# The causal mask added by GpSimd and the gate as the bias of four exponentials, in the recurrence of a two-layer block

## The chip, the cores and the metric

One core of a Trainium2 chip runs the whole program. The metric is device time in microseconds (us) of one launch, over several runs. The engines have the names of the profile: PE is TensorE (matmuls), PEld its weight loads, DVE is VectorE, ACT is ScalarE, POOL is GpSimd, SP the queue that issues nearly all DMAs.

## The reference, cut to what matters

Layer 0 is attention over 256 context tokens and 1024 latents, layer 1 an mLSTM in both directions of time. The change is in layer 1's recurrence, which goes over chunks of 128 tokens:

```python
def step(carry, xs):
    C, n, m = carry
    qq, kk, vv, ig, fg = xs
    b = jnp.cumsum(fg, axis=-1)
    ...
    logD = jnp.where(tril, b[..., :, None] - b[..., None, :] + ig[..., None, :], -jnp.inf)
    m_t = jnp.maximum(b + m[..., None], jnp.max(logD, axis=-1))
    Dm = jnp.exp(logD - m_t[..., None])
    inter = jnp.exp(b + m[..., None] - m_t)
    sqk = jnp.einsum('bhtd,bhsd->bhts', qq, kk) * Dm
    num = jnp.einsum('bhts,bhsd->bhtd', sqk, vv) + inter[..., None] * jnp.einsum('bhde,bhte->bhtd', C, qq)
    den = jnp.sum(sqk, axis=-1) + inter * jnp.einsum('bhd,bhtd->bht', n, qq)
```

The weight `Dm` of key s for query t is exp(g_s - M_t) where s may be seen from t and 0 elsewhere, with g = ig - b and M the running maximum. `qq`, `kk` and `vv` are split into a high and a low part for the products that need precision.

## The kernel before

The recurrence (`phase_b`) works on 32 units: 8 heads times 4 pairs of chunks of the latents, and in a unit on 4 tiles of 128 keys by 128 queries (2 directions d, 2 chunks a). Per unit and in this order the program is written as

- `mid`: the weights times the values (`po<-vh,Eh`, `po<-vl,Eh`, `po<-vh,El`, in `mm3`, L77 to L79) and the state's share (`po<-C,q`, L1262), collected in `num` by ACT (L1258) and DVE (L1263);
- `states`: the chunks' keys and values into the states of the next head: transposes of `x` (`S<-idn,x`, L1205), `ah` high on ACT (L1168) and low on DVE (L1169), products `pc`, the states' update on DVE (L1186);
- a quarter of the next head's output gate (`wh`, `wl` split on POOL, `po<-wh,hT11h` on PE);
- `front` of the unit that follows: q times x (`S<-q,x`, L1229), the load of the negated maxima -M (`nM<-negM_d`, L1234, two DMAs that copy one row to all partitions), the weights E, and their split into Eh and El on POOL (L62, L66);
- `combine` (L1275 to L1289: `e` and `num` on POOL, `r` and `num` on DVE, `num` on ACT, `ms` on POOL) and, a unit later, `back` (transposes of `num`, L1301; `x` on ACT L1304, on DVE L1305, on POOL L1306, then the store `u_d<-x` on SP).

In `front`, before the change, DVE makes `E = min(nM + g, mask)` in four instructions (L1239), with the mask 0 or -1e30, and ACT one exponential over all four tiles (L1242); then DVE multiplies by the scores in PSUM (L1244: mul). `nM` and `E` are tiles with one buffer each: the next unit's `nM` can be loaded only when the last reader of the present one is done, and the next unit's `E` written only when POOL has read the present one for El.

No order is written by hand here. The program is given in the order above, and a scheduler puts each engine's instructions in a fixed order ahead of the run; on the chip each engine, and SP's queue of DMAs, then works strictly through its own list, and a waiting instruction holds all that stand behind it.

Of the kernel before, what the change touches and what calls it, by code (L numbers as in the profile page):

```python
# [19 lines left out]
P = 128  # L20
# [23 lines left out]
# the chunks in the order of each direction: the context first  # L44
# [5 lines left out]
class Ops:  # L50
    """The engines' short forms that the phases share."""
# [20 lines left out]
    def mm3(self, out, lhs, rhs, start, stop):  # L72
        """One step of an accumulated product of two split operands."""
        lh, ll = lhs
        rh, rl = rhs
        mm = self.nc.tensor.matmul
        mm(out, lh, rh, start=start, stop=False)  # L77
        mm(out, lh, rl, start=False, stop=False)  # L78
        mm(out, ll, rh, start=False, stop=stop)  # L79

    def rsqrt(self, out, ms):
        """out = (ms + EPS) ** -0.5"""
        self.nc.gpsimd.tensor_scalar(out, ms, 1.0, EPS, ALU.mult, ALU.add)
        self.nc.gpsimd.tensor_tensor(out, out, self.nhalf[: out.shape[0], : out.shape[1]], ALU.pow)


class Tokens:
    """Features by tokens, as hi and lo, in two tiles of tokens."""
# [12 lines left out]
class Stream:  # L101
    """Tiles of [P, D] in rotation, for the weights and the like of several phases: raw, and split as (hi, lo)."""
# [9 lines left out]
    def pair(self, hold=False):  # L112
        """hold: not to be handed out again before release()."""
# [12 lines left out]
class Modulation0:  # L126
    """Layer 0's cols [P, 2, KT, 2]: A and shift with features on partitions, for (latents, context).

    Parts j of 512 columns, of the shift (0, 1) and of the scale (2, 3)."""
# [16 lines left out]
    def sums(self, j):  # L146
        """The part's sums per partition, on the vector engine; finish() adds them up."""
# [9 lines left out]
    def product(self, j):  # L157
        """The part on the tensor engine."""
# [25 lines left out]
def modulation_rest(nc, ops, A, consts, dst, sp, raw, pair, psum, which):  # L184
    """dst[i]: rows [3, 2, D] in DRAM of layer i: A = norm_pre * (1 + scale), shift, gate * norm_post, for (latents, context).

    Per (i, j) in which two steps for columns j * 512 of shift | scale | gate: the sums on the vector engine, and the rest."""
# [38 lines left out]
def load_row(nc, pool, dst, which, s, name):  # L226
    """A row of the modulation (s: 0 latents, 1 context) on all partitions."""
# [5 lines left out]
def norm_rate(nc, ops, wp, y2, xt):  # L233
    """rsqrt of the rows' mean squares; y2 is written over."""
# [14 lines left out]
def norm(nc, ops, wp, xt):  # L249
    """The rows' rmsnorm."""  # L250
# [12 lines left out]
def shifted(nc, ops, y, shift, hT, f=slice(0, KT)):  # L263
    """hT (hi, lo) = y + shift, of the features' tiles f."""
# [5 lines left out]
def prenorm(nc, ops, wp, xt, row_a, row_s, eng):  # L270
    """rmsnorm(xt) * A + shift"""
# [7 lines left out]
def turn_T(nc, ops, pp, y2, hT, consts):  # L279
    """hT (hi, lo) = transpose of y2."""  # L280
# [3 lines left out]
def layer0(nc, tc, ops, A, consts, mod, dp, ahead, dbg):  # L284
    with ExitStack() as es:
# [10 lines left out]
        with ExitStack() as e1:  # L296
# [4 lines left out]
            with ExitStack() as e2:  # L301
# [18 lines left out]
                def at(t0, n):  # L320
                    """Tokens t0 to t0 + n of the normed input, hi and lo; the first latents lie apart from the others."""
# [101 lines left out]
            def gate(f, wg, wp):  # L423
                """Features f of the gate, on partitions."""
# [11 lines left out]
            with ExitStack() as e2:  # L436
# [11 lines left out]
                def rotary_key():  # L448
                    """The shared rotary key; [hi | lo] of its weights side by side."""
# [67 lines left out]
def queries(nc, ops, A, cT, q_d, g, wp, qp, psum, tab, qf_bufs):  # L517
    """Steps of the queries of heads 4 g to 4 g + 3, into q_d: features of a head lie in steps of four there."""
# [35 lines left out]
def attention(nc, tc, ops, A, consts, cT, kr_d, gate_d, oT_d, last, projected, q_d):  # L554
    """last: what is left to do before it, beside the first head's projections; projected: to be done after the last's."""
    with ExitStack() as es:
# [24 lines left out]
        def proj_v(h):  # L581
            """Values of heads h to h + 3: per head [hi | lo]."""
# [19 lines left out]
        def proj_k(h):  # L602
            """Keys of heads h and h + 1 without the rotary part, which stays in place."""
# [25 lines left out]
        def scores(h, b):  # L629
            """Pieces of a block of 256 queries: scores, and exponentials over their sums, context keys first."""  # L630
# [7 lines left out]
            def part(a, S, j, n):  # L638
                """Exponentials of a part of the keys against its own maximum, and their sum."""
# [22 lines left out]
            def weights(a):  # L662
                """The parts over the sum of all, brought to the largest of their maxima."""
# [20 lines left out]
        def values(h, b, st):  # L684
            """Pairs of steps per two tiles of keys: the transposed weights, and their product with the values."""
# [39 lines left out]
        def projections(h):  # L725
            """Steps beside the head before h."""
# [59 lines left out]
class Out0:  # L786
    """Layer 0's output projection, its norm and residual, and layer 1's normed input, transposed."""
# [13 lines left out]
    def load_o(self, tok, ks):  # L801
        """k-tiles of the first tiles of tokens, or of one."""
# [10 lines left out]
    def ahead(self, W, oT_d):  # L813
        """The first operands."""
# [4 lines left out]
    def run(self, hT, late, following):  # L819
        """late: pools for the last tiles' transposes, which are returned to be done later; following: the next loads."""  # L820
# [3 lines left out]
        with ExitStack() as es:  # L824
# [20 lines left out]
            # while the matrix arrives, three tiles side by side  # L845
# [36 lines left out]
def post(nc, ops, sp, ps, gn, xt, bufs=2, eng="pool"):  # L882
    """xt += rmsnorm(ps) * gn"""
# [9 lines left out]
def feature_weights(nc, ops, W, src):  # L893
    """One tile of features' weights, split."""
# [7 lines left out]
def phase_a(nc, tc, ops, A, consts, mod, hT, S, W, graw, wx0, late):  # L902
    """Layer 1's features: conv branch, its query form, values, and the gates' rows.

    wx0: the first weights; late: the step that completes the last tiles of hT."""
    with ExitStack() as es:
# [26 lines left out]
        for f in range(NF):  # L933
# [5 lines left out]
            # xm, features on partitions  # L939
# [40 lines left out]
            # gates  # L980
# [10 lines left out]
            # values, tokens on partitions  # L991
# [8 lines left out]
            # query form: q against raw conv features as keys  # L1000
# [7 lines left out]
            # the branch gate, for the latents alone  # L1008
# [9 lines left out]
def output_gate(nc, ops, A, S, hT, pools, g, tiles):  # L1018
    """Layer 1's output gate, before its function: steps of a head's weights, and of tiles of latents."""
# [21 lines left out]
def phase_z(nc, tc, ops, A, hT, S, W, tiles):  # L1041
    """Layer 1's output gate, for the latents' first tiles."""
# [583 lines left out]
```

## Time and profile before

| | |
|---|---|
| three runs, us | 2352.1, 2354.07, 2359.23 (median 2354.07) |
| profiled execution: span from first to last instruction | 2352.7 us; its time around the span isn't given |
| instructions | 38304 |
| busy over the span | PE 95%, PEld 83%, DVE 69%, ACT 52%, POOL 47% |
| the recurrence with units of all kinds | about 1687 to 2165 us |
| granted TensorE clock, mean | 0.987 of full speed |

A page of the profile gives busy time and the costliest groups of instructions; the views behind it give, for a stretch, the busy time of each engine, the instructions in order of time, and which engine or DMA ended each wait. "L1239" is line 1239 of the kernel before. Shares over the whole span are means over stages with different limits: in the recurrence alone DVE, not only PE, is busy nearly all the time.

### The profile page before, as it was taken

What the parts mean: (1) busy time and instruction counts of PE and PEld (TensorE: products, weight loads), DVE (VectorE), ACT (ScalarE), POOL (GpSimd) and SP (SyncE); (2) the same over time, 40 slices, a digit from 0 to 9 for tenths busy, and PEclk for the clock granted to TensorE, in tenths of its full rate; (3) what the DMA queues carried; (4) which work ended last, traced back from release to release, by engine and by line L of the source; (5) the groups of instructions that cost most, each with busy time, mean ns of one, the idle gap of its engine ahead of it and who ended that gap; (6) DMA issues with size and microseconds to landing.
All of it is one profiled execution on the core that took longest, in us unless ns stands there. A gap on an engine that the chain in (4) does not pass through costs nothing. (4 is left out here: it accounts for less than half of the span.)

```text
span 2352.7 us, 38304 instructions
## 1 busy us (share of the span) xinstructions
PE 2237.1 (95%) x13462; PEld 1952.1 (83%) x13462; DVE 1620.2 (69%) x3106; ACT 1212.1 (52%) x2935; POOL 1101.9 (47%) x1444
## 2 busy tenths in 40 slices
PE   8998999999999999999999999997999999997998
PEld 4877788998998998887878888887988888896787
DVE  5588499898898997467643444436298999997321
ACT  3512488888788886333222222233366677675111
POOL 3323356656656665562221111145546666656321
PEclk9999999999999999999999999999999999999999
DMA  7066422222311212543443333333634555545531
GB/s 260 28 210 219 142 79 78 71 59 67 88 45 58 82 54 89 178 157 124 137 144 117 126 115 109 111 132 103 208 106 152 161 163 173 169 124 177 171 125 54
DMA packets 189464, 292.26 MB, mean 124 GB/s; under 512 B 14108, under 2 KB 134812, under 8 KB 188888
## 3 DMA queue, kind: packets, MB, share of 16 engines
q1 hardware_dynamic: 188744, 287.97, 38.7%
q8 instruction: 107, 1.75, 0.3%
q0 software_dynamic: 528, 1.84, 0.2%
q14 instruction: 85, 0.70, 0.1%
HBM read 199.13 MB, written 90.62 MB: 123 GB/s over the span
## 5 line engine op out<-in xcount | busy, mean ns | idle before, releaser
L677 POOL TENSOR_SCALAR P<-P,sc,rs 128x512 f32<-128x512 f32 (+1 forms) x384 | 271.0, 720 | 160.4 <-DVE rs L675 109.1
L643 ACT ACTIVATE P<-S,nm 128x512 f32<-128x512 f32 (+1 forms) x416 | 254.2, 613 | 55.4 <-DVE nm L642 45.2
L642 DVE TENSOR_REDUCE nm<-S 128x1 f32<-128x512 f32 (+1 forms) x416 | 236.7, 578 | 19.8 <-PE S L79 18.8
L66 DVE TENSOR_TENSOR PTl<-tps,PTh 128x512 fp32r<-128x512 f32 x336 | 227.9, 680 | 10.5 <-ACT PTh L58 8.4
L58 ACT CAST PTh<-tps 128x512 fp32r<-128x512 f32 x336 | 197.0, 587 | 27.1 <-PE tps L694 24.3
L694 PE MATMUL tps<-idn,P 128*128 128x128 f32 x1344 | 202.0, 273 | 1.0 <-DVE PTl L66 0.7
L62 POOL TENSOR_SCALAR wh<-raw 128x512 fp32r<-128x512 f32 (+1 forms) x96 | 85.9, 907 | 242.0 <-PE xps L78 165.0
L66 DVE TENSOR_TENSOR wl<-raw,wh 128x1024 fp32r<-128x1024 f32 (+2 forms) x51 | 77.4, 1526 | 148.4 <-POOL wh L62 136.4
L694 PEld LDWEIGHTS tps<-idn,P 128*128 128x128 f32 x1344 | 156.5, 141 | 7.2 <-issue 1.0
L705 PEld LDWEIGHTS po<-PTh,V 128*128 128x128 f32 x672 | 119.3, 190 | 31.1 <-ACT o L714 11.4
L705 PE MATMUL po<-PTl,V 128*128 128x256 f32 x672 | 136.4, 284 | 7.5 <-DVE PTl L66 6.5
L1262 PE MATMUL po<-C,q 128*128 128x258 f32 x512 | 136.2, 388 | 6.1 <-ACT num L1258 6.1
L705 PE MATMUL po<-PTh,V 128*128 128x256 f32 x672 | 139.1, 288 | 2.7 <-ACT o L714 2.4
L77 PE MATMUL xps<-hT10h,wh 128*128 128x512 f32 (+1 forms) x384 | 139.4, 363 | 0.0
L78 PE MATMUL xps<-hT10l,wh 128*128 128x512 f32 (+1 forms) x384 | 137.4, 358 | 0.0
L79 PE MATMUL xps<-hT10h,wl 128*128 128x512 f32 (+1 forms) x384 | 137.3, 358 | 0.0
L974 DVE SCALAR_TENSOR_TENSOR xc<-xp,cw,xc 128x1282 f32<-128x1282 f32 x64 | 105.9, 1655 | 12.7 <-ACT xc L972 11.2
L705 PEld LDWEIGHTS po<-PTl,V 128*128 128x128 f32 x672 | 104.8, 189 | 9.0 <-DVE PTl L66 7.8
L1262 PEld LDWEIGHTS po<-C,q 128*128 128x128 f32 x512 | 89.9, 194 | 15.1 <-ACT num L1258 6.9
L1186 DVE SCALAR_TENSOR_TENSOR C<-C,decay,pc 128x258 f32<-128x258 f32 x224 | 100.1, 472 | 2.3 <-PE pc L79 2.0
L77 PE MATMUL xps<-hT11h,wh 128*128 128x512 f32 x256 | 99.9, 391 | 1.1 <-ACT hT11h L58 1.1
L79 PE MATMUL xps<-hT11h,wl 128*128 128x512 f32 x256 | 100.2, 391 | 0.0
(658 smaller groups left out, 7306.6 us busy)
## 6 DMA issues: line engine op xcount, KB each, us to landing
raw<-in_w_og SPq DMA_DIRECT2D x32, 512.0 KB, 4.2
qT<-q_d SPq DMA_DIRECT2D x16, 960.0 KB, 6.6
adaw<-in_ada_w SPq DMA_DIRECT2D x48, 256.0 KB, 3.3
q_d<-qs SPq DMA_DIRECT2D x24, 512.0 KB
xt<-in_xcat SPq DMA_DIRECT2D x20, 512.0 KB, 3.6
v_d<-vt SPq DMA_DIRECT2D x16, 640.0 KB
v<-v_d SPq DMA_DIRECT2D x40, 256.0 KB, 3.6
x<-xcT_d SPq DMA_DIRECT2D x40, 256.0 KB, 3.7
```

Source lines behind the costliest of these rows:

```text
L58: self.nc.scalar.copy(out, x)
L66: e.tensor_tensor(out, x, hi.bitcast(F32), ALU.subtract)
L77: mm(out, lh, rh, start=start, stop=False)
L78: mm(out, lh, rl, start=False, stop=False)
L79: mm(out, ll, rh, start=False, stop=stop)
L642: nc.vector.tensor_reduce(nm, S, axis=AX.X, op=ALU.max, negate=True)
L643: nc.scalar.activation(p, S, AF.Exp, bias=nm, accum_out=sm)
L677: nc.gpsimd.tensor_scalar(pt[j], pt[j], sc[:, j : j + 1], r[:, 3:], ALU.mult, ALU.mult)
L694: nc.tensor.transpose(pt[:, kk * 256 + a * P : kk * 256 + (a + 1) * P], src, consts["idn"])
L705: nc.tensor.matmul(po, Vs[h][:, k].rearrange("p a d -> p (a d)"), PT[i][:, kk * 256 : kk * 256 + 256], start=k == 0 and i == 0, stop=k == ...
L974: nc.vector.scalar_tensor_tensor(xc, xp[:, j : j + CONV_W], cw[:, f, j : j + 1], xc, ALU.mult, ALU.add)
L1262: nc.tensor.matmul(pi[:, :VW], qa, C[:, k], start=k == 0, stop=k == 1)
```

## The change

DVE's four instructions are gone. POOL adds the mask to -M, in place and for all four tiles at once (the mask is read twice by a broadcast), and ACT makes four exponentials of one tile each, with the column of g as the bias. The values are the same: a masked place has exp(-1e30) = 0. The rest of the diff only takes comments and docstrings away.

```diff
             nM = lp.tile([P, 2, U], F32, name="nM", bufs=1)
             for d in range(2):
                 nc.sync.dma_start(nM[:, d], S["negM"][d, h : h + 1, c * U : (c + 1) * U].partition_broadcast(P))
+
+            nv = nM.rearrange("p d (a s) -> p d a s", a=2)
+            nc.gpsimd.tensor_tensor(nv, nv, mask.unsqueeze(2).to_broadcast([P, 2, 2, P]), ALU.add)
             E = lp.tile([P, 2, 2, P], F32, name="E", bufs=1)
             for d in range(2):
                 for a in range(2):
                     gcol = cols[d][:, 2 * c + a, 3, h : h + 1]
-                    nc.vector.scalar_tensor_tensor(
-                        E[:, d, a], nM[:, d, a * P : (a + 1) * P], gcol, mask[:, d], ALU.add, ALU.min
-                    )
-            nc.scalar.activation(E, E, AF.Exp)
+                    nc.scalar.activation(E[:, d, a], nv[:, d, a], AF.Exp, bias=gcol)
             wide = ps[:, :, :P].unsqueeze(1).to_broadcast([P, 2, 2, P])
             nc.vector.tensor_tensor(E, wide, E, ALU.mult)
```

In the lists below a number behind a tile's name tells one tile of that name from another.

POOL's list between El of a head's last unit (El_21418) and the split of the next head's first (Eh_21604). Before:

```order
L66 TENSOR_TENSOR El_21418<-E_21410,Eh_21417 128x512
L66 TENSOR_TENSOR vl_21404<-v_20196,vh_21403 128x516
L1306 TENSOR_TENSOR x_20422<-x_20422,sz_21443 128x512
L1200 MEMSET v_21912 128x2
L1201 MEMSET v_21912 128x2
L1275 COPY e_21827<-gcol0_17373 128x2
L1275 COPY e_21827<-gcol1_17374 128x2
L1284 TENSOR_TENSOR num_21243<-num_21243,og_21421 128x256 x2
L62 TENSOR_SCALAR Eh_21604<-E_21597 128x512
L66 TENSOR_TENSOR El_21605<-E_21597,Eh_21604 128x512
```

And now:

```order
L66 TENSOR_TENSOR El_21418<-E_21411,Eh_21417 128x512
L1306 TENSOR_TENSOR x_20422<-x_20422,sz_21443 128x512
L66 TENSOR_TENSOR vl_21404<-v_20196,vh_21403 128x516
L1237 TENSOR_TENSOR nM_21809<-nM_21809,mask_18583 128x512
L1275 COPY e_21827<-gcol0_17373 128x2
L1275 COPY e_21827<-gcol1_17374 128x2
L1200 MEMSET v_21912 128x2
L1201 MEMSET v_21912 128x2
L1284 TENSOR_TENSOR num_21243<-num_21243,og_21421 128x256 x2
L83 TENSOR_SCALAR ms_21423<-ms_21423 128x2
L84 TENSOR_TENSOR ms_21423<-ms_21423,nhalf_67 128x2
L62 TENSOR_SCALAR Eh_21604<-E_21598 128x512
```

The add that is put in belongs to the unit after the one whose Eh follows (nM_21809 is for a later E than E_21598), it stands three rows behind El, and `ms` has moved ahead of Eh.

The same list behind El of a head's first unit (El_20747), where a quarter of the output gate's weights (`wh2`, `wl2`) is split. Before:

```order
L66 TENSOR_TENSOR El_20747<-E_20739,Eh_20746 128x512
L83 TENSOR_SCALAR ms_20565<-ms_20565 128x2
L84 TENSOR_TENSOR ms_20565<-ms_20565,nhalf_67 128x2
L66 TENSOR_TENSOR vl_20733<-v_20181,vh_20732 128x516
L1200 MEMSET v_21282 128x2
L1201 MEMSET v_21282 128x2
L62 TENSOR_SCALAR wh2_20794<-raw_20793 128x512 x2
L1306 TENSOR_TENSOR x_19579<-x_19579,sz_20772 128x512
L66 TENSOR_TENSOR wl2_20795<-raw_20793,wh2_20794 128x512 x2
L1275 COPY e_21212<-gcol0_17373 128x2
L1275 COPY e_21212<-gcol1_17374 128x2
L1284 TENSOR_TENSOR num_20598<-num_20598,og_20750 128x256
```

And now:

```order
L66 TENSOR_TENSOR El_20747<-E_20740,Eh_20746 128x512
L1306 TENSOR_TENSOR x_19579<-x_19579,sz_20772 128x512
L66 TENSOR_TENSOR vl_20733<-v_20181,vh_20732 128x516
L1237 TENSOR_TENSOR nM_21194<-nM_21194,mask_18583 128x512
L62 TENSOR_SCALAR wh2_20794<-raw_20793 128x512 x2
L1200 MEMSET v_21282 128x2
L1201 MEMSET v_21282 128x2
L1275 COPY e_21212<-gcol0_17373 128x2
L1275 COPY e_21212<-gcol1_17374 128x2
L66 TENSOR_TENSOR wl2_20795<-raw_20793,wh2_20794 128x512 x2
L1284 TENSOR_TENSOR num_20598<-num_20598,og_20750 128x256 x2
```

Again the add stands behind `x` and `vl`, with the gate weights' splits and `num` behind it.

DVE's list around `x_20179<-S_21232` (L1305), whose end frees a PSUM buffer, in a head's last unit. Before:

```order
L1283 SCALAR_TENSOR_TENSOR num_21000<-num_21000,r_21211 128x256
L1169 SCALAR_TENSOR_TENSOR ahl_21143<-v_21039,gcol1_17374,ahh_21142 128x258
L1239 SCALAR_TENSOR_TENSOR E_21410<-nM_21407,gcol0_17373,mask_18583 128x128 x2
L1239 SCALAR_TENSOR_TENSOR E_21410<-nM_21407,gcol1_17374,mask_18583 128x128 x2
L1305 SCALAR_TENSOR_TENSOR x_20179<-S_21232,hns_18585,x_20179 128x256 x2
```

And now:

```order
L1186 SCALAR_TENSOR_TENSOR C9_21094<-C1_20911,decay_17375,pc_21087 128x258
L1283 SCALAR_TENSOR_TENSOR num_21000<-num_21000,r_21211 128x256 x2
L1169 SCALAR_TENSOR_TENSOR ahl_21128<-v_21054,gcol0_17373,ahh_21127 128x258
L1305 SCALAR_TENSOR_TENSOR x_20179<-S_21232,hns_18585,x_20179 128x256 x2
L1186 SCALAR_TENSOR_TENSOR C6_21109<-C13_21079,decay_17375,pc_21102 128x258
```

The four L1239 that stood ahead of L1305 are gone, and one L1169 and one L1186 have moved behind it.

## Rows read from the trace of the kernel before

**Rows 1.** Stretches: length; busy us of PE, PEld, DVE, ACT, POOL; clock; DMA share:

```profile
1687.00:2165.00 478.00, 437.19 (x3025) 402.74 (x3025) 434.69 (x929) 323.01 (x807) 299.92 (x435) 0.98 0.52 158
1750.00:2100.00 350.00, 328.78 (x2340) 306.70 (x2339) 327.62 (x711) 246.97 (x630) 229.74 (x344) 0.99 0.53 161
1903.25:1923.48 20.23, 19.32 (x143) 17.82 (x141) 17.18 (x39) 12.86 (x31) 14.43 (x25) 1.00 0.53 187
1923.48:1934.57 11.09, 8.52 (x63) 7.98 (x62) 10.99 (x25) 8.66 (x24) 6.04 (x10) 1.00 0.42 108
1934.57:1945.10 10.53, 10.53 (x79) 10.05 (x79) 10.33 (x25) 6.14 (x17) 6.46 (x10) 1.00 0.47 141
1945.10:1960.88 15.78, 15.20 (x108) 14.11 (x107) 15.35 (x33) 12.49 (x31) 11.69 (x18) 1.00 0.67 195
```

**Rows 2.** What PE waited for, 1750 to 2100 us (total, times, longest):

```profile
PE S L1205 <- issue: 10.8, 5, 2.6
PE po L77 <- DVE num L1263: 4.0, 7, 0.6
PE pc L79 <- DVE thl L66: 2.9, 5, 0.6
```

**Rows 3.** Groups of DVE, 1687 to 2165 us: busy us, mean ns | idle before:

```profile
L1169 DVE SCALAR_TENSOR_TENSOR ahl<-v,gcol,ahh 128x258 fp32r<-128x258 f32 x141 | 88.1, 627 | 7.9 <-PE S L1205 4.5 <-ACT ahh L1168 3.1
L1239 DVE SCALAR_TENSOR_TENSOR E<-nM,gcol,mask 128x128 f32<-128x128 f32 x127 | 60.4, 530 | 1.3 <-DMA nM<-negM_d 1.0 <-POOL El L66 0.4
```

**Rows 4.** Line 1239 alone: duration ns min/median/max:

```profile
L1239 DVE SCALAR_TENSOR_TENSOR E<-nM,gcol,mask x128: 334/340/4407, 1686.4 to 2144.0; 128x128 f32<-128x128 f32 x128
```

**Rows 5.** In order of time, DVE and PE, 1924 to 1927 us (start, us):

```profile
1924.56 1.51 DVE L1239 SCALAR_TENSOR_TENSOR E<-nM,gcol,mask 128x128 f32<-128x128 f32 x4
1925.99 0.86 DVE L1305 SCALAR_TENSOR_TENSOR x<-S,hns,x 128x256 f32<-128x256 f32 x2
...
1926.96 0.41 PE L1205 MATMUL S<-idn,x 128*128 128x128 f32 x2 [2.57 <-issue]
```

**Rows 6.** In order of time, POOL and DVE, near 1902 us:

```profile
1901.97 1.27 POOL L66 TENSOR_TENSOR El<-E,Eh 128x512 fp32r<-128x512 f32 x1
...
1902.40 1.13 DVE L1169 SCALAR_TENSOR_TENSOR ahl<-v,gcol,ahh 128x258 fp32r<-128x258 f32 x1 [0.20 <-ACT ahh L1168]
```

**Rows 7.** Groups of ACT, whole span: busy us, mean ns:

```profile
L643 ACT ACTIVATE P<-S,nm 128x512 f32<-128x512 f32 x256 | 178.4, 697 | 39.4 <-DVE nm L642 37.4 <-DVE rs L675 0.4
L643 ACT ACTIVATE P<-S,nm 128x256 f32<-128x256 f32 x160 | 76.2, 478 | 16.0 <-DVE nm L642 7.7 <-PE tps L694 5.8 <-DVE rs L673 0.8
L1242 ACT ACTIVATE E<-E 128x512 f32<-128x512 f32 x32 | 20.2, 631 | 25.8 <-DVE E L1239 19.2 <-DVE r L1277 6.5
```

**Rows 8.** The DMAs of nM: issue, ns, and time to landing, us:

```profile
L1234 SPq DMA_DIRECT2D nM<-negM_d x64: 320/378/1306, 1681.8 to 2128.9; - x64
...
DMA to landing us min/median/max: 3.3/4.3/7.6
```

**Rows 9.** POOL in order of time, 1933 to 1946 us:

```profile
1933.29 1.28 POOL L66 TENSOR_TENSOR El<-E,Eh 128x512 fp32r<-128x512 f32 x1
1934.53 1.49 POOL L66 TENSOR_TENSOR vl<-v,vh 128x516 fp32r<-128x516 f32 x1
1935.97 1.34 POOL L1306 TENSOR_TENSOR x<-x,sz 128x512 f32<-128x512 f32 x1
...
1942.06 0.64 POOL L1284 TENSOR_TENSOR num<-num,og 128x256 f32<-128x256 f32 x1 [0.36 <-DVE num L1283]
1943.06 0.62 POOL L62 TENSOR_SCALAR Eh<-E 128x512 fp32r<-128x512 f32 x1 [0.37 <-DVE E L1244]
...
1945.45 0.71 POOL L84 TENSOR_TENSOR ms<-ms,nhalf 128x2 f32<-128x2 f32 x1
```

**Rows 10.** In order of time: PE's use of El and Eh, POOL's Eh:

```profile
1945.00 0.28 PE L79 MATMUL po<-vh,El 128*128 128x258 f32 x1
...
1958.04 0.79 POOL L62 TENSOR_SCALAR Eh<-E 128x512 fp32r<-128x512 f32 x1
```

## The prediction

> **What bounds the kernel now.** I read busy time by stretch first, then PE's waits, then DVE's groups, then the order of time inside four units. In the recurrence (478 us) PE is busy 437 us and DVE 435; ACT has 323 and POOL 300 [rows 1]. So two engines are nearly full, and neither can be called the bound from these shares alone. The reader is to see next that in the steady part, 1750 to 2100 us, PE stands idle 350 - 328.8 = 21 us, and that 10.8 + 4.0 + 2.9 = 17.7 us of its listed waits have to do with DVE [rows 1, 2]. Two of these lines name DVE. The first, on L1205, names nobody ("issue"), but in order of time one sees it: four L1239 run on DVE from 1924.56, L1305 from 1925.99 to 1926.85, and PE goes on at 1926.96 after 2.57 us without work [rows 5]. L1305 reads the PSUM buffer that PE wants for the transposes. So PE is the pace, with DVE's queue as nearly its only brake.
>
> The last four stretches of [rows 1] each go from the end of one unit's El to the end of the next's; I call them one to four (20.2, 11.1, 10.5, 15.8 us, 57.6 in all, a head's worth). PE's idle time lies mostly in stretch two: 8.5 us busy of 11.1.
>
> POOL looks free, with 120 of 350 us idle. But its El is used as soon as it is there: in stretch three El ends at 1945.10 and PE's product with it is listed from 1945.00 (matmul starts and ends are modelled) [rows 1, 10].
>
> **What leaves DVE.** Per unit four L1239 of 0.340 us (median), 128 in all: 43.5 us. They were busy 60.4 us (127 in the stretch), so some 17 us more was waiting inside the instruction [rows 3, 4]. That is 1.9 us of DVE per unit, 12.5% of its 478 us. As a gain it counts only where PE waited. Of the 10.8 us on L1205, in five waits, I take the 1.5 us of the four L1239 ahead of L1305 from each: 7.5. Of the other 6.9 us I take half, since those waits also depend on products and on ACT. That is 11 us in six heads, 13 in the seven that run beside a next head. Bounds: nothing, if PE merely waits elsewhere, and 17.7 x 7/6 = 21 us.
>
> **What comes to ACT.** One exponential of 0.631 us goes, four of 128 elements come. Exponentials with a bias column took 0.697 us for 512 elements and 0.478 for 256 [rows 7]: 0.219 for 256 elements less, so about 0.37 for 128, and 1.5 us for four. Those two rows read PSUM and also sum, so this is an estimate; the bounds are 0.63 (no more than now) and 4 x 0.478 = 1.9. ACT gains 0.85 us per unit, 27 us over 32, against 478 - 323 = 155 idle. I price its load at nothing, and the chain's 1.5 us goes into the loop below.
>
> **What comes to POOL.** The add has the shape of El (two inputs in SBUF, 128 x 512): 1.28 us [rows 9], 41 us over 32 units, 31 in the steady part. More matters than its length. It waits for the two DMAs of nM, and everything behind it on POOL waits with it: the gate weights' splits, `e`, `num`, and the next Eh. nM has one buffer. Its load for the unit after next starts when the present unit's exponentials have read it, and these start when El of the unit ahead has released E. From El's end to the landing I count 0.3 us until ACT begins (an estimate), 1.5 for the exponentials, 0.4 for the second of the two issues and 4.3 to landing [rows 8]: 6.5 us. With landings from 3.3 to 7.6 us it is 5.5 to 9.8. Before the change the same load had a whole unit, 10.5 to 20 us, before DVE read it.
>
> In the lists that the change section shows, only `x` and `vl` stand between El and the add: 1.34 + 1.49 = 2.8 us [rows 9]. POOL then waits 3.7 us. Over all units of the steady part the work placed there is 3.3 us in the mean by the same prices, so 24 x 3.2 = 77 us of waiting plus 31 of adds: 108 us into 120 us of idle time. POOL becomes as full as PE, and only what overlaps with its old waits is free.
>
> Stretch by stretch: in three the add ends at 6.5 + 1.28 = 7.8 us; `e` 0.3, two `num` 1.3, `ms` 0.9 (now ahead of Eh), Eh 0.62 and El 1.28 make 12.2 against 10.5 [rows 1, 9]. In the heads where the add stands behind the `num` pair, the pair's end at 1942.70 (8.1 us in) plus 1.28, 0.9 and 1.9 gives 12.2 as well. PE had no slack there: 1.65 us lost. In four: 7.8, then two `wh` 1.25, `e` 0.3, two `wl` 2.6, two `num` 1.3, so Eh starts at 13.3 against 12.9 (1958.04) [rows 10]: 0.4 to 0.5 lost. In one and two the same count ends no later than now (18.5 and 9.7 us), so I take nothing. Loss: 2.15 us per head, 15 over seven.
>
> **Sum.** 15 - 13 = +2 us on a span of 2352.7, so 2354.7. The median of the runs is 1.4 us above that span, and I add it: **2356 us**.
>
> **A rule against the change.** Row first: El ran on POOL from 1901.97 to 1903.24, and a DVE instruction with two SBUF inputs (L1169) that began at 1902.40 ended only at 1903.53, 1.13 us instead of the group's mean of 0.627 [rows 3, 6]. The add is 41 us more of such POOL time on 300 [rows 1], 14% more chances to be blocked; L1169 stays with 141 instructions. By the bound that every add blocks one DVE instruction for its whole length, DVE would get 41 of its 60 us back. The Trainium skill, page "SBUF — State Buffer", section "Who interferes with whom", says that a DVE instruction with two SBUF inputs and a GpSimd instruction that reads SBUF exclude each other on a shared port, and that whichever comes second blocks fully. The row agrees with it. By that rule the removed L1239 were themselves victims (mean 530, median 340 ns), so I take the net as still clearly lighter for DVE.
>
> **Rivals.**
> - DVE's relief shows, POOL's new wait hides: **faster**, about 2338 us. POOL's 120 idle us take the 108, if its old waits (for `num`, `r` and E of DVE) end during the wait for nM. Then stretch three loses little and the 13 to 21 us of PE's waits go: 2354 - 16. For it: DVE gets `num` and `r` ready earlier. Against: stretch three has no slack.
> - The wait for nM takes over as the pace: **slower**, about 2372 us. It decides from about 7.3 us between El and landing on: each further us lengthens nearly every unit, 24 us per us in the steady part by the count above, 28 in all. At 7.3 it is the 15 us above and 0.8 x 28 = 22 more, less the 13, plus some overlap: +18. For it: SP issues the load in its own strict order, behind stores that wait for POOL's `x`; the landing reaches 7.6 us. Against: the median is 4.3.
> - The blocked port eats the relief: **slower**, about 2366. If DVE gets back 41 of 60 us, only a third of the 13 us gain is left, 4, against the 15 lost: +11.
> - The change does nothing else: the four exponentials replace one, and if they cost 1.9 us the loop is 0.4 us longer. That lies inside the range.
>
> **How the numbers follow.** Forecast, 2356, within 2347 to 2361: 0.38. DVE's relief wins: 0.28. The wait for nM: 0.27. The port: 0.07. A measurement of this kernel can tell about 0.3%, 7 us. So faster 0.28, same 0.38, slower 0.34. The range of 8 in 10 reaches from the gain's upper bound without a loss, 2354 - 21 = 2333, to the loss without a gain and 0.5 us more of wait, 2354 + 15 + 14 = 2383; I cut both a little: 2335 to 2380.
>
> **What the profile after would show.** DVE busy 50 to 60 us less over the recurrence, and no 2.6 us wait of PE on L1205. ACT's L1242 at 0.3 to 0.4 us. POOL's add near 1.28 us with an idle time before it that DMA nM ended, 2 to 4 us per unit, some 100 us in all; POOL's old waits for DVE smaller. PE's waits ended by POOL (Eh, El), near zero now, at some 15 us. If the add's idle time is below 1 us per unit, the loop is wrong and the time is faster. If it is above 5, or PE's waits for Eh and El exceed 25 us, it is slower. What could make all of this wrong is the order: it was set anew for every engine in the recurrence, and I have followed it on POOL and at one place of DVE alone.

## The result and the profile after

The changed kernel took 2395.98 us (median), the kernel before 2356.12 beside it: a ratio of 1.0184, 95% interval 1.0168 to 1.0200. The forecast was 2356 with a range to 2380. So the change costs 40 us, and the prediction was wrong. The profiled execution has a span of 2394.3 us. Times below are medians; one of e7's ten executions took 6821.91 us, and without it e7's median is 2359.95.

The first two stretches of [rows 1] after the change, and then the stretch from 1687 us to the end, before and after:

```profile
1687.00:2165.00 478.00, 423.93 (x2903) 393.56 (x2904) 367.59 (x763) 319.33 (x850) 309.07 (x438) 0.96 0.47 146
1750.00:2100.00 350.00, 310.25 (x2133) 288.18 (x2133) 271.41 (x563) 234.35 (x633) 236.75 (x341) 0.96 0.49 150
```

```profile
1687.00:2352.70 665.70, 613.68 (x3788) 544.53 (x3788) 482.25 (x987) 357.46 (x866) 346.15 (x474) 0.98 0.48 147
1687.00:2394.30 707.30, 629.72 (x3788) 558.89 (x3788) 443.43 (x860) 374.03 (x961) 384.36 (x506) 0.96 0.44 139
```

The recurrence now goes on for 41 us longer (the last L1262 starts at 2206.8 us, before at 2165.8), so a stretch with fixed ends holds less of its work. Counted to the end, DVE has 482.3 - 443.4 = 39 us less to do, less than the 50 to 60 of the forecast: the L1239 took 60.4 us, but L1169 takes 11 us more than before. PE, which had 21 us without work in the steady part, now has 40. To the end, with the same 3788 matmuls, its idle time grows by 26 us and its busy time by 16, which together are the 42 us of span; the granted clock falls from 0.98 to 0.96.

The groups and issues of the new operations, and the waits of PE (1750 to 2100 us, the view of [rows 2]):

```profile
L1237 POOL TENSOR_TENSOR nM<-nM,mask 128x512 f32<-128x512 f32 x32 | 43.3, 1354 | 78.2 <-DMA nM<-negM_d 56.8 <-ACT num L1258 7.5 <-ACT thh L58 6.2
L1242 ACT ACTIVATE E<-nM,gcol x128: 384/388/412, 1689.0 to 2183.1; 128x128 f32<-128x128 f32 x128
L1234 SPq DMA_DIRECT2D nM<-negM_d x64: 320/422/1137, 1681.3 to 2166.7; - x64
DMA to landing us min/median/max: 3.0/4.1/5.5
...
PE po L1262 <- ACT num L1258: 12.4, 9, 3.2
PE S L1301 <- ACT num L1289: 7.8, 5, 2.6
PE pc L77 <- ACT thh L58: 7.7, 2, 5.2
PE pc L77 <- ACT C L1177: 5.4, 6, 1.8
PE S L1229 <- DMA q<-qT_d: 2.9, 3, 1.7
PE po L78 <- POOL vl L66: 0.9, 2, 0.6
PE po L77 <- DVE num L1263: 0.7, 2, 0.5
```

The first four lines are near the forecast: the add at 1.35 us with 78.2 / 32 = 2.4 us of idle POOL in front of it (56.8 of the 78.2 us ended by the load), the exponentials 0.388 us, the landing near 4.3 us. PE's waits for DVE are nearly gone. Yet no wait of PE names POOL's Eh or El, where the forecast put the loss. They name ACT: 12.4 + 7.8 + 7.7 + 5.4 = 33 us.

How POOL's wait becomes ACT's and then PE's is seen at the longest case, in order of time on POOL, then ACT, then PE (start, us):

```profile
1800.11 1.26 POOL L1237 TENSOR_TENSOR nM<-nM,mask 128x512 f32<-128x512 f32 x1 [6.78 <-DMA nM<-negM_d]
1801.33 1.32 POOL L1284 TENSOR_TENSOR num<-num,og 128x256 f32<-128x256 f32 x2
...
1795.73 0.37 ACT L1258 COPY num<-po 128x258 f32<-128x258 f32 x1
1802.08 0.42 ACT L1285 ACTIVATE num<-num 128x256 f32<-128x256 f32 x1 [5.98 <-POOL num L1284]
...
1802.49 0.57 ACT L58 CAST thh<-S 128x512 fp32r<-128x512 f32 x1
...
1797.62 0.28 PE L79 MATMUL po<-vh,El 128*128 128x258 f32 x1
1803.11 0.58 PE L77 MATMUL pc<-ahh,thh 128*128 128x258 f32 x1 [5.21 <-ACT thh L58]
```

POOL stands 6.78 us in front of the add. Behind the add, in POOL's list, is `num` (L1284). ACT's square of it (L1285) stands 5.98 us, and behind that, in ACT's list, is the cast `thh`, which has nothing to do with `num` but which PE waits for: 5.21 us. Each engine does its list in order, so one late load reaches three engines through two instructions that happen to stand behind one another. The Trainium skill, page "TensorE: Matmul & The Clock Gate", section "Architectural detail: the array is 16× 32×32, not 1× 128×128", says that the queues of ScalarE and VectorE are strictly first in, first out, and GpSimd's so on each of its cores; the rows above agree with it.

It is not a single case. Between 1750 and 2165 us PE has seven waits of 2.5 us or more, ending at 1757.96, 1803.11, 1837.73, 1930.64, 1996.34, 2055.11 and 2113.99 us, 21.8 us in all. In order of time each leads back in the same way: PE waits for ACT, ACT for `num` or `ms` on POOL, and POOL has just stood 1.4 to 6.8 us for the load in front of an add. PE's shorter waits were not all followed.

ACT's wait for `num` doubles. 1687 to 2165 us, before and then after:

```profile
ACT num L1285 <- POOL num L1284: 19.3, 21, 2.0
```

```profile
ACT num L1285 <- POOL num L1284: 42.0, 22, 6.0
```

### The profile page after: what moved, and what is told of

Its sections match the earlier page's. It is cut to its first block, busy times and chain, and to the rows that moved or that the text cites. A ratio compares the mean times of both kernels' runs of the same rounds, so it can differ in the third digit from the quotient of the medians.

```text
span 2394.3 us, 38338 instructions
## 1 busy us (share of the span) xinstructions
PE 2257.5 (94%) x13462; PEld 1970.5 (82%) x13462; DVE 1577.4 (66%) x2978; ACT 1229.0 (51%) x3031; POOL 1142.9 (48%) x1476
## 5 line engine op out<-in xcount | busy, mean ns | idle before, releaser
L1262 PE MATMUL po<-C,q 128*128 128x258 f32 x512 | 144.1, 403 | 17.3 <-ACT num L1258 17.1
L77 PE MATMUL xps<-hT10h,wh 128*128 128x512 f32 (+1 forms) x384 | 140.0, 365 | 0.0
L79 PE MATMUL xps<-hT10h,wl 128*128 128x512 f32 (+1 forms) x384 | 137.9, 359 | 0.0
L1169 DVE SCALAR_TENSOR_TENSOR ahl<-v,gcol,ahh 128x258 fp32r<-128x258 f32 x144 | 102.1, 713 | 35.7 <-ACT ahh L1168 31.8
L77 PE MATMUL pc<-ahh,thh 128*128 128x258 f32 x288 | 100.7, 352 | 19.8 <-ACT thh L58 7.7
L1262 PEld LDWEIGHTS po<-C,q 128*128 128x128 f32 x512 | 93.2, 202 | 28.5 <-ACT num L1258 19.8
L974 DVE SCALAR_TENSOR_TENSOR xc<-xp,cw,xc 128x1282 f32<-128x1282 f32 x64 | 105.0, 1641 | 12.7 <-ACT xc L972 11.2
L1186 DVE SCALAR_TENSOR_TENSOR C<-C,decay,pc 128x258 f32<-128x258 f32 x224 | 101.0, 474 | 2.9 <-PE pc L79 1.8
```

The lines of the kernel that those rows point to most:

```text
L974: nc.vector.scalar_tensor_tensor(xc, xp[:, j : j + CONV_W], cw[:, f, j : j + 1], xc, ALU.mult, ALU.add)
L1262: nc.tensor.matmul(pi[:, :VW], qa, C[:, k], start=k == 0, stop=k == 1)
```

## The experiments

The theories. **A**: POOL's list stands at the wait for nM, and what stands behind it is late. **B**: the four exponentials load ACT too much. **C**: POOL's 1.28 us of work, or its port, is the cost. Later **A'** (the round trip through nM: exponentials, load, add, on whichever engine stands in it), **E** (the add's place in the list), **F** (all time in which POOL's list is taken up, waiting or working, counts alike). e1, e2, e13, e14 and e16 leave the mask and g out of the computation and make the exponential of -M times 0.001 (with a bias of zeros, `zero`, in all but e13), so they show times alone. Every kernel's lists are ordered anew, and the line numbers move by a few lines between them. The loss is the median minus that of the kernel before, measured beside it.

| run | median us | ratio, 95% interval | loss us |
|---|---|---|---|
| changed kernel | 2395.98 | 1.0184, 1.0168 to 1.0200 | 39.9 |
| e1 wait alone | 2364.31 | 1.0056, 1.0039 to 1.0072 | 10.7 |
| e2 work alone, ahead of Eh | 2371.15 | 1.0075, 1.0060 to 1.0090 | 17.5 |
| e3 add in place on DVE | 2395.01 | 1.0176, 1.0161 to 1.0191 | 41.4 |
| e4 add into E | 2355.54 | 1.0010, 1.0001 to 1.0020 | 1.9 |
| e5 split exponential only | 2358.72 | 1.0033, 1.0020 to 1.0046 | 6.0 |
| e6 two nM | 2391.02 | 1.0165, 1.0151 to 1.0180 | 38.3 |
| e7 add into its own tile | 2360.42 | 1.0032, 1.0022 to 1.0043 | 7.7 |
| e8 add into E on DVE | 2363.67 | 1.0053, 1.0038 to 1.0068 | 10.9 |
| e9 in place, twice | 2403.15 | 1.0214, 1.0194 to 1.0235 | 50.8 |
| e10 into E, twice | 2382.21 | 1.0128, 1.0106 to 1.0151 | 29.9 |
| e11 into E, two E | 2356.20 | 1.0017, 1.0005 to 1.0028 | 3.9 |
| e12 into E, `num` scaled on DVE | 2370.13 | 1.0082, 1.0064 to 1.0101 | 17.8 |
| e13 relief alone | 2355.95 | 1.0009, 0.9999 to 1.0019 | 0.9 |
| e14 relief, four exponentials | 2342.41 | 0.9953, 0.9939 to 0.9967 | -12.7 |
| e15 into E, one and a half | 2361.20 | 1.0032, 1.0019 to 1.0046 | 6.1 |
| e16 in place, half | 2374.24 | 1.0088, 1.0070 to 1.0105 | 19.1 |
| e17 into E, half on each engine | 2363.14 | 1.0033, 1.0021 to 1.0045 | 8.5 |

**e1, the wait without the work.**

```diff
-nc.gpsimd.tensor_tensor(nv, nv, mask..., ALU.add)
+nc.gpsimd.tensor_tensor(nv[:, :, :, :1], nv[:, :, :, :1], mask[:, :, :1]..., ALU.add)
-nc.scalar.activation(E[:, d, a], nv[:, d, a], AF.Exp, bias=gcol)
+nc.scalar.activation(E[:, d, a], nv[:, d, a], AF.Exp, bias=zero, scale=1e-3)
```

> The changed kernel with GpSimd's mask addition cut to one column of each tile (128x4 instead of 128x512), and the exponentials of the raw maxima with scale 0.001 and a zero bias: the mask and g are left out, GpSimd still waits for each nM at the same place in its order, but the 1.28 us of work and its traffic are gone. Theory A (GpSimd's queue stands at the wait for the load, and num, which ScalarE needs, stands behind it): about 41 us of work leave an engine that waits there anyway, so 2385 to 2397 us, with GpSimd still idle over 50 us before L1239 and ScalarE still waiting some 35 us for GpSimd's num. Theory B (the four exponentials load ScalarE too much): 2390 to 2397. Theory C (the 1.28 us of GpSimd work, or its port, is the loss): 2340 to 2360.

2364 us lies in no theory's range: 21 us below A's, 4 above C's. POOL's group at the wait (busy, mean | idle before):

```profile
L1239 POOL TENSOR_TENSOR nM<-nM,mask 128x4 f32<-128x4 f32 x31 | 6.8, 219 | 57.8 <-DMA nM<-negM_d 42.2 <-ACT num L1260 6.6 <-ACT thh L58 5.9
```

57.8 of the 78.2 us of waiting are still there, but three quarters of the loss are not. The wait does not cost 40 us by itself.

**e2, the work without the wait.**

```diff
-nc.gpsimd.tensor_tensor(nv, nv, mask..., ALU.add)
-nc.scalar.activation(E[:, d, a], nv[:, d, a], AF.Exp, bias=gcol)
+nc.scalar.activation(E[:, d, a], nv[:, d, a], AF.Exp, bias=zero, scale=1e-3)
 nc.vector.tensor_tensor(E, wide, E, ALU.mult)
+nc.gpsimd.tensor_tensor(idle, E, mask..., ALU.add)
```

> The other half: GpSimd adds the mask to E into a tile that nobody reads, just ahead of its split of E, and does not touch nM; the exponentials read nM itself, with scale 0.001 and a zero bias, so the mask and g are left out. GpSimd's 128x512 addition is there 32 times (1.28 us) in a worse place than in the changed kernel, right in front of Eh, but its wait for nM is gone. Theory A (the wait in GpSimd's queue): 2345 to 2365 us, ScalarE's wait for GpSimd's num back near that of the kernel before. Theory B (ScalarE's load): 2390 to 2400. Theory C (the work): 2390 or more.

2371 us lies between A's range and those of B and C. This add stands between DVE's product and Eh, so this is no clean price of the work; e4 and e7 place it better.

**e3, e4 and e8: another engine, another target.**

```diff
-nc.gpsimd.tensor_tensor(nv, nv, mask..., ALU.add)
+nc.vector.tensor_tensor(nv, nv, mask..., ALU.add)    # e3
+nc.gpsimd.tensor_tensor(E, nv, mask..., ALU.add)     # e4
+nc.vector.tensor_tensor(E, nv, mask..., ALU.add)     # e8
-nc.scalar.activation(E[:, d, a], nv[:, d, a], AF.Exp, bias=gcol)
+nc.scalar.activation(E[:, d, a], E[:, d, a], AF.Exp, bias=gcol)    # e4, e8
```

> The changed kernel with the mask addition, the whole of it, on VectorE. GpSimd has neither work nor wait; VectorE gets back about 32 x 0.6 = 19 us of the 80 us that the change took from it, and stands itself at the wait for nM. Theory A, that GpSimd's queue is the one that hurts: 2345 to 2370 us, as VectorE's work is queued behind the load in its turn, with idle VectorE of 20 us or more ended by the load. Theory B (ScalarE's load): 2390 to 2400. Theory C (GpSimd's work): 2335 to 2350.

> The changed kernel with one word changed: GpSimd's addition writes into E instead of over nM, and the exponentials work on E in place. The whole computation is done. nM is then free as soon as the addition has read it, so that the next unit's load has a whole unit (some 15 us) to land before the next addition, which itself stands right behind El, when E is free. Theory A: GpSimd's idle time ended by nM falls from 57 us to under 10, ScalarE's wait for num falls with it, and the time to 2335 to 2360 us. Theory B (ScalarE's load) and theory C (GpSimd's work): unchanged, 2385 to 2400.

> The run that adds into E, with the one addition of 128x512 on VectorE (about 0.6 us a unit in place of four steps of 0.53) and GpSimd as in the kernel before; the whole computation is done. VectorE is relieved by some 48 us instead of 80, GpSimd by 41 us against the run on GpSimd. If VectorE's work sets the pace, as the gain of the forecast had it: 2335 to 2348 us. If TensorE with its own work and ScalarE's longer list leave no more: 2350 to 2358. If VectorE, standing at the wait for nM again, loses as it did with the addition in place: 2385 or more.

e3 loses as much as the changed kernel with POOL out of it, which C and the A of POOL alone cannot give. The groups of e3 and of e4:

```profile
L1237 DVE TENSOR_TENSOR nM<-nM,mask 128x512 f32<-128x512 f32 x32 | 23.0, 719 | 85.1 <-DMA nM<-negM_d 85.1
```

```profile
L1238 POOL TENSOR_TENSOR E<-nM,mask 128x512 f32<-128x512 f32 x32 | 42.4, 1326 | 5.0 <-issue 3.5
```

In e3 DVE stands 85 us at the load (36 of it once, at the start, where the kernel before stands 34 us too). In e4 the same POOL add waits 5.0 us, and the loss is gone; ACT's four exponentials are there too, so B falls. The same move helps on DVE, 41 to 11 us (e8, between its second case and its third). What e3 and the changed kernel share is the round trip, hence A'. The route to PE is another in e3: PE's largest waits there are for ACT's `num` (19.5 us) and for `C`, the states' update on DVE (19.3).

**e5, ACT's load alone**: the one exponential of the kernel before, split in four.

```diff
-nc.scalar.activation(E, E, AF.Exp)
+nc.scalar.activation(E[:, d, a], E[:, d, a], AF.Exp, bias=zero)    # for each d, a
```

> The kernel before with its one exponential of 128x512 cut into four of 128x128 with a bias column of zeros; the four VectorE steps stay and GpSimd does nothing new. It adds to ScalarE alone what the change adds there, about 4 x 0.385 - 0.70 = 0.84 us a unit, 27 us in all. Theory B (this load makes the loss): 2380 us or more. Theory A' (the loss is the round trip through nM, its load and the addition, with the engine that stands in it): 2352 to 2362.

6 us, not 40.

**e6 and e7: a second nM, and a tile of its own for the sum.**

```diff
-nM = lp.tile([P, 2, U], F32, name="nM", bufs=1)
+nM = lp.tile([P, 2, U], F32, name="nM", bufs=2)                    # e6
-nc.gpsimd.tensor_tensor(nv, nv, mask..., ALU.add)
+G = lp.tile([P, 2, 2, P], F32, name="G", bufs=1)                   # e7
+nc.gpsimd.tensor_tensor(G, nv, mask..., ALU.add)                   # e7
+nc.scalar.activation(E[:, d, a], G[:, d, a], AF.Exp, bias=gcol)    # e7
```

> The changed kernel with two tiles of nM in place of one, the addition in place on GpSimd as it was. A simple view, that a second buffer hides the load: GpSimd's idle time ended by nM falls to under 15 us, 2345 to 2365 us. Theory A': the order of the instructions uses the second tile to put each addition one unit further ahead; its load still waits for the exponentials that lie right behind the same El, and so it lands as late with respect to GpSimd's list: idle time ended by nM still 45 us or more, 2385 to 2400 us.

> The changed kernel with the addition, still on GpSimd and between the same El and Eh of its list, written into a tile of its own that the exponentials read; E stays as it was. nM is free as soon as the addition has read it, so its load no longer begins behind the exponentials. It differs from the changed kernel in the round trip alone, while the run that adds into E also moved the addition behind El. Theory A': idle time ended by nM under 15 us, 2345 to 2365 us. If the place in GpSimd's list was what that run mended (theory E): 2380 to 2400.

Both times are in the range of A'. POOL's groups in e6 and in e7:

```profile
L1237 POOL TENSOR_TENSOR nM<-nM,mask 128x512 f32<-128x512 f32 x32 | 42.8, 1337 | 78.1 <-DMA nM<-negM_d 68.2 <-ACT ahh L1168 6.5 <-issue 3.4
```

```profile
L1238 POOL TENSOR_TENSOR G<-nM,mask 128x512 f32<-128x512 f32 x31 | 40.8, 1317 | 20.7 <-ACT E L1243 20.6
```

With a second nM the add is listed one unit further ahead, its load still starts behind the exponentials of the same moment, and the idle time is the same 78 us. In e7 the add stands between the same El and Eh as in the changed kernel, but nM is free as soon as it is read: its line names no DMA, and 32 us come back. So it is the round trip, not the place in the list (E).

**e9 and e10: the work twice.** In e9 the add in place stands twice; in e10 the mask is added into E as in e4 and then once more to E.

> The changed kernel with GpSimd's addition in place done twice (the mask is added a second time; a masked weight is zero either way): 32 x 1.28 = 41 us more GpSimd work between the landing of nM and the exponentials. Theory A' (the loss is a round trip of load and addition that GpSimd's list stands in): taking this work away gave back 32 us of the 40, so putting it in once more costs 25 to 42 us: 2420 to 2440 us. If the addition's work only filled idle time: 2393 to 2402.

> The run that adds into E, with the addition into E done twice on GpSimd: the same 41 us more GpSimd work, with no load to wait for. Theory A': without the load the engine has slack for it and the same work costs less than half of what it costs in place, 5 to 18 us: 2360 to 2374. If the work itself sets the time wherever it stands (theory C): 2385 to 2400.

Both lie outside the range of A', in opposite directions: 11 us more than the changed kernel in place, 28 more than e4 into E. In place the second add can stand apart from the first (at 1846.09 and 1848.96 us in one unit, with other work between), and the load's wait falls from 78.2 to 67.3 us:

```profile
L1237 POOL TENSOR_TENSOR nM<-nM,mask 128x512 f32<-128x512 f32 x32 | 42.5, 1328 | 67.3 <-DMA nM<-negM_d 56.3 <-ACT ahh L1168 6.3 <-issue 3.5
```

Into E nothing is waited for:

```profile
L1238 POOL TENSOR_TENSOR E<-nM,mask 128x512 f32<-128x512 f32 x31 | 41.5, 1339 | 1.3
L1239 POOL TENSOR_TENSOR E<-E,mask 128x512 f32<-128x512 f32 x32 | 42.3, 1323 | 0.6
```

The second 42 us of work cost 28 us, twice the 14.6 of the first (e4 against e14, below). The work is not free anywhere.

**e11 and e12: what is left after e4.** Both begin from e4: with two tiles of E; and with the first scaling of `num` on DVE.

```diff
+E = lp.tile([P, 2, 2, P], F32, name="E", bufs=2)                           # e11
-nc.scalar.activation(n0, n0, AF.Copy, scale=r[:, 0, a : a + 1])
+nc.vector.tensor_scalar(n0, n0, r[:, 0, a : a + 1], None, ALU.mult)        # e12
```

> The run that adds into E, with two tiles of E in place of one, so that the addition and the exponentials of the next unit need not wait for El. If the single E still cost something there: 2342 to 2351 us. If nothing is left in that loop: 2352 to 2360, the same as with one. It leaves nothing out of the computation.

> The run that adds into E, which relieves VectorE by some 22 us of busy time where PE is in the loop and puts 20 us on ScalarE, with the first scaling of num (64 steps of 128x256) moved from ScalarE to VectorE, where the step before it and the step after it stand. ScalarE waited 28 us in 350 for that r. If ScalarE's list is what eats VectorE's relief: 2335 to 2348 us. If TensorE's own work leaves no more: 2350 to 2358. If VectorE fills up again: 2360 or more.

Neither gains: a second E changes nothing, and DVE, given work again, costs 16 us over e4.

**e13 and e14: the gain by itself.**

```diff
-nc.vector.scalar_tensor_tensor(E[:, d, a], nM[...], gcol, mask[:, d], ALU.add, ALU.min)
-nc.scalar.activation(E, E, AF.Exp)
+nc.scalar.activation(E, nv, AF.Exp, scale=1e-3)                                  # e13
+nc.scalar.activation(E[:, d, a], nv[:, d, a], AF.Exp, bias=zero, scale=1e-3)      # e14, for each d, a
```

> The kernel before without its four VectorE steps: one exponential of the raw maxima with scale 0.001, so the mask and g are left out; GpSimd and ScalarE do what they did before. It is the relief of VectorE (some 80 us over the phase) by itself. The forecast's gain term: 13 us off, 2336 to 2343. If VectorE's steps were waited for by nobody in the end: 2350 to 2356. It also says how far the 40 us of the changed kernel are a gain lost and a loss added.

> The same, with the exponential in four pieces of 128x128 and a bias column of zeros (scale 0.001; the mask and g are left out): VectorE relieved, ScalarE with the changed kernel's load, GpSimd with neither work nor wait. The forecast priced ScalarE at nothing: the same time as the relief alone. The run that only split the exponential cost 6 us: then 4 to 8 us over the relief alone. If ScalarE is what PE waits for once VectorE is out of the way (theory B in part): 10 us or more over it.

The relief alone gains nothing; with the exponential in four pieces it gains 12.7 us, though the same split cost 6 in the kernel before. No case foretold that. The lists differ: ACT's idle time in front of the first scaling of `num` is 78.6 us in e13 and 23.4 in e14:

```profile
L1277 ACT ACTIVATE num<-num,r 128x256 f32<-128x256 f32 x64 | 29.3, 504 | 78.6 <-DVE r L1274 78.6
```

```profile
L1281 ACT ACTIVATE num<-num,r 128x256 f32<-128x256 f32 x64 | 29.0, 500 | 23.4 <-DVE r L1278 23.4
```

Whether that order is the whole of the 13 us was not tried.

**e15, e16 and e17: half sizes.**

```diff
 nc.gpsimd.tensor_tensor(E, nv, mask..., ALU.add)
+nc.gpsimd.tensor_tensor(E[:, 1], E[:, 1], mask[:, 1:]..., ALU.add)          # e15
-nc.gpsimd.tensor_tensor(nv[:, :, :, :1], nv[:, :, :, :1], mask[:, :, :1]..., ALU.add)
+nc.gpsimd.tensor_tensor(nv[:, 1], nv[:, 1], mask[:, 1:]..., ALU.add)        # e16
-nc.gpsimd.tensor_tensor(E, nv, mask..., ALU.add)
+for d, eng in enumerate((nc.vector, nc.gpsimd)):                            # e17
+    eng.tensor_tensor(E[:, d], nv[:, d], mask[:, d : d + 1]..., ALU.add)
```

(e15 and e17 begin from e4, e16 from e1.)

> The run that adds into E, with the mask added once more to one half of E (128x256) on GpSimd. Theory F: the loss goes by how long GpSimd's list is taken up, by work or by standing in front of nM alike, summed over the 32 units. The runs so far, as time taken up and loss over the kernel before: 47 us and 2 (into E), 62 and 8 (own tile), 65 and 11 (wait alone), 86 and 30 (into E twice), 121 and 38 to 40 (changed; two nM), 152 and 51 (in place twice). Here some 68 to 71 us are taken up: 10 to 18 us over the kernel before, 2362 to 2371 us. If work counts only by the whole addition, in a straight line between one and two of them: 2366 to 2372, which is not told apart; if the first half more is free: 2353 to 2358.

> The run with the wait alone, with the addition in place on 128x256 in place of 128x4 (scale 0.001 and a zero bias in the exponentials, so the mask and g are left out): between the wait alone (11 us over the kernel before) and the changed kernel (40). Theory F: about 22 us of work and 60 to 70 of waiting, 82 to 92 us taken up, as much as with the addition into E done twice: 26 to 34 us over the kernel before, 2378 to 2387 us. If waiting counts for less than work: 12 to 24 us over it.

> A candidate with the whole computation: the run that adds into E, with one direction's half of the addition (128x256) on VectorE and the other on GpSimd. Without either the wait or the addition the kernel took 2342 us; the whole addition into E costs 13 us over that on GpSimd and 21 on VectorE. If the cost of GpSimd's work is convex, as the runs with 42, 68 and 84 us of it (2, 6 to 8 and 30 us over the kernel before) have it, half of it on each engine costs less than either: 2346 to 2353 us, at or below the kernel before. If each half costs its share, 2357 to 2361; if two hand-overs in place of one add their own: 2362 or more.

F falls. e16's group:

```profile
L1239 POOL TENSOR_TENSOR nM<-nM,mask 128x256 f32<-128x256 f32 x32 | 23.7, 741 | 78.2 <-DMA nM<-negM_d 58.6 <-ACT num L1260 6.6 <-DMA sz<-sz_d 3.4
```

23.7 + 78.2 = 102 us of POOL cost 19 us there, while e10's 84 us of pure work cost 30: waiting counts for less than work. e15 lost less than its 10 to 18, and e17, the candidate, lies in its third case: no version with the whole computation beat the kernel before.

## Why the prediction was wrong

With e14 as the kernel with neither add nor wait, the change falls into parts:

| POOL has | loss over the kernel before | over e14 |
|---|---|---|
| neither (e14) | -12.7 | 0 |
| the wait, 6.8 us of work (e1) | 10.7 | 23.4 |
| the add, no wait for the load (e4; e7) | 1.9; 7.7 | 14.6; 20.4 |
| both (changed kernel) | 39.9 | 52.6 |

**The gain, 13 us: right in size, unproved in its reason.** Without POOL's part the change gains 12.7. But the forecast had it from DVE's relief, which gained nothing alone (e13). PE's waits for DVE did shrink as said, but that the size agrees is luck as far as these runs show.

**ACT at nothing: near.** 0.388 us an exponential against 0.37 foretold; the split alone costs 6 us in one order and belongs to a gain in the other.

**The add and the wait: near in length, wrong in price.** The wait and its cause came as worked out, its parts not quite. The loop from El's end to the start of the next add takes 7.4 us in the mean of the 23 units of the steady part, not 6.5; no row showed the 0.3 us until ACT begins, which is 0.5 in the mean. Work and other waits take 7.4 - 2.4 = 5.0 us between El and the wait, against 3.3 counted, so POOL's wait is 56 us in the steady part and not 77; the adds are the 31 us forecast. The step that failed is the price, "Stretch by stretch": it followed the delay through POOL's Eh and El alone and had 2.15 us lost per head, 15 over seven. Add and wait measured 52.6 us over e14. The wait by itself cost 23 us and the work by itself 15 to 20; together they cost 9 to 15 more than their sum. The route was another, too: not POOL's Eh and El, but `num`, which the forecast named among what is queued behind the add and then did not follow to ACT, where it holds `thh` and PE. The forecast also had no term for longer matmuls, which are 16 of the 42 us of span, at a granted clock of 0.96 against 0.98.

**The rivals.** "DVE's relief shows" forecast 2338 us for a new wait that hides; it did not hide, and e14, without add and wait, took 2342. "The wait for nM takes over as the pace" had the right mechanism (e6, e7), and its onset of 7.3 us between El and landing was passed, if barely: 7.4 us. The landing itself stayed at 4.1 us. By its own count that is about 2375 us, so it too priced the wait too low. "The blocked port": the mean of L1169, 627 ns in [rows 3], is 708 ns in the changed kernel, but 703 in e14 without any add. First the changed kernel, then e14:

```profile
L1169 DVE SCALAR_TENSOR_TENSOR ahl<-v,gcol,ahh 128x258 fp32r<-128x258 f32 x141 | 99.4, 708 | 32.6 <-ACT ahh L1168 28.6 <-PE S L1205 3.4
```

```profile
L1171 DVE SCALAR_TENSOR_TENSOR ahl<-v,gcol,ahh 128x258 fp32r<-128x258 f32 x141 | 98.0, 703 | 11.9 <-ACT ahh L1170 7.2 <-PE S L1207 4.3
```

So the mean rose without the added POOL work. In e4, where the add stands behind El and the loss is gone, it is longer still:

```profile
L1169 DVE SCALAR_TENSOR_TENSOR ahl<-v,gcol,ahh 128x258 fp32r<-128x258 f32 x141 | 115.2, 819 | 14.2 <-ACT ahh L1168 9.8 <-PE S L1205 3.4 <-DMA og<-og_d 0.9
```

819 - 703 = 116 ns times 141 is 16 us of DVE, about e4's 14.6 over e14. That the two are one thing was only argued. In the traces the length of an L1169 goes with the POOL work that it meets in time. In the changed kernel 14 overlap an add and take 858 ns in the mean, 88 overlap other POOL work (783), and 39 overlap none (483); in e4 30 overlap an add (1111) and 29 none (481); in e14 54 overlap none (481) and 87 other work (841). The rule that the forecast took from the Trainium skill, page "SBUF — State Buffer", section "Who interferes with whom", that such instructions exclude each other, agrees with these means. The forecast's bound was one blocked instruction for every add: e4 comes near it with 30 L1169 on 32 adds, the changed kernel has 14.

**What stays open.** The price of POOL's time is neither additive nor a straight line (e9, e10, e15), and every edit sets the lists anew, which alone moved up to 13 us (e13, e14). No run held the order fixed. Nor is ACT's wait for `num` a measure of the loss: from 1687 to 2210 us it is 43.8 us in the changed kernel, but 25.3 in e9, which loses more, and 45.4 in e12, which loses 17.8. That e1's wait and e4's work together cost more than their sum was measured, and not explained.

## What to carry to other kernels

An in-place step on a freshly loaded buffer turns a hidden load into a round trip, because the load cannot start before the last reader of the sum; writing the sum into a tile that is there anyway lets the load run ahead (here 40 us of loss became 2), while a second buffer for the load brought 2 us of the 40. When a wait is put into a list, follow each instruction queued behind it to its reader, and from there what is queued behind that reader: the idle time of the engine that waits says little about the price. And an engine's idle share is no room to let: the 42 us of work cost 15 to 20 us on an engine that had been idle for a third of the steady part.

## What was unexpected of the hardware

The stalls also cost TensorE its clock. Stretches around the case above (busy us of PE, PEld, DVE, ACT, POOL; granted clock):

```profile
1790.00:1798.00 8.00, 7.90 (x57) 7.36 (x56) 5.32 (x15) 6.07 (x15) 2.94 (x8) 1.00 0.35 105
1798.00:1803.00 5.00, 0.00 (x0) 0.00 (x0) 0.00 (x0) 0.92 (x4) 2.84 (x4) 0.84 0.74 264
1803.00:1806.00 3.00, 2.89 (x11) 2.70 (x12) 1.24 (x3) 1.60 (x6) 3.00 (x4) 0.50 0.30 101
1806.00:1812.00 6.00, 6.00 (x39) 5.70 (x38) 4.81 (x10) 3.01 (x7) 4.18 (x6) 0.81 0.58 173
```

After 5 us without a matmul the clock stands at 0.50, the lower level of 1.2 GHz, and it is 0.81 over the 6 us that follow. A product of 128x258 that took 0.28 us ahead of the wait (L79, in the rows of the longest case) takes 0.58 us behind it (L77, whose median is 0.34). Over the phase, 1687 to 2200 us, the mean of a matmul rises. Before and after (busy us, mean ns; 12 of the 512 now lie behind 2200 us):

```profile
L1262 PE MATMUL po<-C,q 128*128 128x258 f32 x512 | 136.2, 388 | 6.1 <-ACT num L1258 6.1
L77 PE MATMUL pc<-ahh,thh 128*128 128x258 f32 x288 | 96.6, 337 | 3.1 <-DVE C L1186 2.8 <-ACT C L1177 0.2
```

```profile
L1262 PE MATMUL po<-C,q 128*128 128x258 f32 x500 | 140.1, 402 | 17.3 <-ACT num L1258 17.1
L77 PE MATMUL pc<-ahh,thh 128*128 128x258 f32 x288 | 100.7, 352 | 19.8 <-ACT thh L58 7.7 <-ACT C L1177 7.2 <-DVE C L1186 4.3
```

For these two groups that is 512 x 14 + 288 x 15 ns = 11.5 us of the 16 us by which PE's busy time grew. A forecast that counts lost waits alone leaves this out.
